# Smaller TensorE tiles and regrouped products in a hybrid decoder layer on one core

## Chip, cores and metric

The kernel runs on one core of a Trainium2 chip. The metric is the device time of one execution in microseconds (us). Three executions of the kernel before took 877.32, 881.16 and 882.83 us; the median is 881.16 us.

## The reference, cut to what matters

One layer of a decoder is computed for a prompt of 1024 tokens and for 8 sample sequences of 8 tokens each. The normalised input is projected once, and three groups of heads use the result:

- **RWKV-7** (4 heads of 64): a matrix state per head is updated token by token. With `S` the state, each step computes `sa = S @ (-kk)`, then `S = S*w + sa (kk*a)^T + v k^T`, and the output `y = S @ r`.
- **MLA** (8 heads): causal attention over the prompt. For the samples, attention over 2048 cached positions per sequence and over the sequence's own 8 new tokens: `s_past` and `s_new` are concatenated before the softmax.
- **Memory cross-attention** (4 heads): not touched here.

The gated outputs go through one output projection, a residual and a final RMSNorm. All inputs and outputs are float32.

## The kernel before

**Order of the work.** The program is written as Python generators that are stepped in turn, but what each engine runs in which order is set at compile time by a planner. It takes the instructions with the priority of their emission, holds one back while its operands or its buffer are not ready by the planner's own estimate of time, and fills in with others. So one engine's order in the trace is not the order of the file: products of different lines are found mixed.

**The RWKV part** (`rwkv_seg`, called from `phase_a`). The prompt is cut into 8 segments of two 64-token chunks, and the samples make a ninth of one chunk. Two head pairs (`hp`) times two chunks (`ch`) give the four index pairs `HP`, counted by `c`. A head pair fills 128 partitions; `H[0]` are partitions 0 to 63, `H[1]` 64 to 127, and `G` is the same in reverse. Three segments are in work at a time, in three stages (the `yield`s). Stage 1 computes the scores `AS` of keys against keys and queries (L742 to L750): per half `h`, four products of 64 rows by 128 columns, 128 moving columns each, into one PSUM bank (tag `rwa`, one buffer), then a VectorE multiply with the mask. A triangular inverse follows (L753 to L785, on VectorE and GpSimd, and L809 to L828 with 64x64 products). Stage 3 carries the state from chunk to chunk: `pW` from L846 and L850, `W`, `pU` from L856, `VU`, `pS` from L863, the next `S`. Then the outputs `py` (bank tag `rwd`, one buffer) are summed from a "tokens" product (L883, 128 rows by 64 columns) and a "state" product (L885, 64 by 64), pair by pair of `HP`, the two parts in alternating order, and normalised (L890 to L899), transposed (L903) and stored.

A product of two float32 operands shows in the trace as two passes: two weight loads and two matmuls. The tile shape of a matmul is the number of rows and of columns of the 128x128 array that it uses, 64*128 for instance.

While RWKV runs, TensorE also has other work: the input projection (`chunks` and `natural`, lines L181 to L183 of the helper `mm3`), and from about 400 us on the first two head pairs of the prompt's MLA.

**Prompt MLA** (`mla_prompt`). For each of four head pairs and each block `qb` of 128 queries, `scores` computes for each head `a` the scores against the keys up to the block's end, `n = 128 (qb+1)`. They are cut into parts of up to 512 keys, one bank each: three products per part (L1410 to L1412, float32r, at least 256 columns wide), a mask product on the last part (L1414), a VectorE maximum per part (L1415), a ScalarE exponential with a sum per part (L1420). For `n = 640` the parts are 512 and 128 keys, and the second is computed 256 wide. `outputs` transposes (L1440) and multiplies with `V` (L1451).

**Sample MLA** (`mla_sample`). The scores of the new tokens (L1211 to L1215) are made once: for each of four pairs of sequences, two products of 128 rows by 64 columns and then one of 64 by 128, all into one bank. Then 16 rounds over the cached pages follow, with scores (L1259 to L1261) and outputs (L1272) each.

Of the kernel before, what the change touches and what calls it, by code (L numbers as in the profile page):

```python
# [18 lines left out]
P = 128  # L19
# [684 lines left out]
def rwkv_seg(tc, A, g, sp, ps, s):  # L704
# [4 lines left out]
    nc = tc.nc  # L709
# [5 lines left out]
    n2 = 2 * nch  # L715
    mi = 1 if smp else 0
    T = lambda shape, tag, bufs=1, dt=F32: sp.tile(shape, dt, name="r_" + tag, tag=tag, bufs=bufs)
    bank = lambda tag="rwb": ps.tile([P, 512], F32, name="rwps", tag=tag, bufs=1)
    ga = lambda t, n: t.rearrange("p (a n) -> p a n", n=n)
    H = (slice(0, 64), slice(64, 128))  # L720
    G = H[::-1]
    HP = [(hp, ch) for hp in range(2) for ch in range(nch)]


    i, c0, t0 = (4, 0, 0) if smp else (s // 2, 2 * (s % 2), 128 * (s % 2))
    tok = SEQ if smp else s * N
    KR = T([P, 2, 2, 128], "KR", 3)[:, :, :nch]
    nc.sync.dma_start(out=KR, in_=g.kr_d[i, :, :, c0:c0 + nch])
    KN = T([P, 2, 2, 128], "KN", 2)[:, :, :nch]
# [10 lines left out]


    AS = T([P, 2, 4, 128], "AS", 3)[:, :, :n2]  # L742
    pa = [ga(bank("rwa"), 128) for h in range(2)]
    for c, (hp, ch) in enumerate(HP):
        for h in range(2):
            nc.tensor.matmul(pa[h][:, c], lhsT=KN[H[h], hp, ch], rhs=KR[H[h], hp, ch], start=True, stop=True)
    m = r.maskA[:, mi].rearrange("p a t -> p (a t)")
    for h in range(2):
        nc.vector.tensor_tensor(out=AS[:, h], in0=pa[h][:, :n2], in1=m.unsqueeze(1).broadcast_to([P, n2, 128]),
                                op=ALU.mult)  # L750


# [5 lines left out]
    for h in range(2):  # L758
        nc.vector.scalar_tensor_tensor(out=F[G[h], :n2], in0=AS[G[h], h, :, 32:64], scalar=r.bm[G[h], 4:5],
                                       in1=AS[G[h], h, :, 0:32], op0=ALU.mult, op1=ALU.add)  # L760
# [11 lines left out]
    for i in range(1, 16):  # L772
        n = i + 1
        nc.vector.tensor_tensor(out=tmp[:, :, :, :n], in0=NAv[:, i, :, :n].unsqueeze(2).broadcast_to([P, 2, 2, n]),  # L774
                                in1=Tl[:, :, :, :n].rearrange("p c b t -> p b c t"), op=ALU.mult)
# [5 lines left out]
    for b in range(4):  # L781
        nc.gpsimd.tensor_scalar(
            out=Tm[:, :, b * 16:(b + 1) * 16].rearrange("p c (r a) -> p r a c", a=2),
            in0=Tc.rearrange("p a r c -> p r a c")[:, :, :, :n2], scalar1=r.bm[:, b:b + 1], scalar2=1.0,
# [4 lines left out]
    VU = T([P, 2, 4, 64], "VU", 2)[:, :, :n2]  # L789
# [16 lines left out]
    fl = lambda t: t.rearrange("p a n -> p (a n)")  # L806
# [25 lines left out]
    if smp:  # L832
        py = rwkv_sample_state(tc, A, g, bank, T, KR, nat, AS, VU, Z)
    Ss = []
    for ch in range(0 if smp else nch):
        S = r.S
        q = 2 * s + ch
# [5 lines left out]
        for hp in range(2):  # L843
            c = hp * nch + ch
            for h in range(2):
                nc.tensor.matmul(pW[G[h], hp], lhsT=AS[H[h], h, c, 0:64], rhs=VU[H[h], h, c], start=True,  # L846
                                 stop=S is None)
# [5 lines left out]
        for hp in range(2):  # L853
            c = hp * nch + ch
# [5 lines left out]
        for hp in range(2):  # L860
            c = hp * nch + ch
# [10 lines left out]
        Ss.append(S)  # L872
    if not smp:
        py = ga(bank("rwd")[:, :64 * n2], 64)
        for c, (hp, ch) in enumerate(HP):

            S = Ss[ch]
            parts = ["tokens", "state"] if S is not None else ["tokens"]
            for k, part in enumerate(parts[::-1] if c % 2 else parts):
                a, b = k == 0, k == len(parts) - 1  # L880
                for h in range(2):
                    if part == "tokens":
                        nc.tensor.matmul(py[H[h], c], lhsT=AS[:, h, c, 64:128], rhs=VU[:, h, c], start=a, stop=b)  # L883
                    else:
                        nc.tensor.matmul(py[H[h], c], lhsT=KR[H[h], hp, ch, 64:128], rhs=S[H[h], hp], start=a,  # L885
                                         stop=b)

    st, mv = T([P, 4, 6], "st", 2), T([P, 4, 2], "mv", 2)
    yn = T([P, 4, 64], "yn", 2)
# [255 lines left out]
def mla_sample(tc, A, g, sp, banks):  # L1145
    nc = tc.nc
    bank = lambda: banks("ps", 1)
    obank = lambda: banks("po", 1)
    ident = g.ident
    fl = lambda t: t.rearrange("p h t -> p (h t)")  # L1150
# [19 lines left out]
    for hp in range(4):  # L1170
        w = sp.tile([P, 2, 256], F32, name="swq", tag="a2", bufs=4)
        nc.sync.dma_start(out=w, in_=A["wuq"][:, hp])
        for a in range(2):
            for k in range(2):
                nc.tensor.matmul(pq[:, a, hp], lhsT=w[:, k, a * P:(a + 1) * P], rhs=g.cqs[:, k], start=k == 0,
                                 stop=k == 1)
# [7 lines left out]
    qlat = sp.tile([P, 8, 8, 8], F32, name="sqlat")  # L1184
# [3 lines left out]
    for a in range(2):  # L1188
        pp = bank()
        nc.tensor.matmul(pp[:, :256], lhsT=sel[:, a], rhs=Q[:, a].rearrange("p h n -> p (h n)"), start=True, stop=True)  # L1190
        for rep in range(4):
            q, i = slice(rep * 32, rep * 32 + 32), rep % 2
# [17 lines left out]
    ps = bank()  # L1210
    for q in range(4):  # L1211
        for i in range(2):
            b, rows = 2 * q + i, slice(i * 64, i * 64 + 64)
            nc.tensor.matmul(ps[rows, q * 64:(q + 1) * 64], lhsT=fl(qlat[:, b]), rhs=g.cks, start=True, stop=False)
        nc.tensor.matmul(ps[:, q * 64:(q + 1) * 64], lhsT=qrf[0:64, q], rhs=g.kps, start=False, stop=True)  # L1215
    nc.vector.tensor_tensor(out=Pn, in0=ps[:, :256].rearrange("p (a b) -> p a b", a=4), in1=smask, op=ALU.add)
    nc.vector.tensor_reduce(out=nm[:, :, 4], in_=Pn, axis=AX.X, op=ALU.max, negate=True)
    pt = bank()
# [85 lines left out]
def mla_prompt(tc, A, g, sp, ps, more):  # L1304
# [4 lines left out]
    def bank():  # L1309
        turn[0] += 1  # L1310
        if more and turn[0] % 2:
            return more[0].tile([P, 512], F32, name="mT", tag="mT2", bufs=1)
        return ps.tile([P, 512], F32, name="mT", tag="mT", bufs=1)
# [31 lines left out]
    for hp in range(4):  # L1345
# [46 lines left out]
        def scores(qb):  # L1392
            c = slice(qb * P, (qb + 1) * P)
            n = (qb + 1) * P
            nm = sp.tile([P, 2, 3], F32, name="mnm", tag="mnm", bufs=3)
            sm = sp.tile([P, 2, 3], F32, name="msm", tag="msm", bufs=3)
            nh = (n + 511) // 512
            r = 2 if nh == 2 else 0
            Pts = []
            for a in range(2):  # L1400
                Pt = sp.tile([P, SEQ], F32, name="mP", tag="mP", bufs=3)
                S = []
                for i in range(nh):
                    c0 = i * 512
                    m = min(512, n - c0)
                    w = slice(c0, c0 + max(256, m))
                    s = sbank()
                    o = s[:, :max(256, m)]
                    last = i == nh - 1
                    nc.tensor.matmul(o, lhsT=qh[a][:, c], rhs=kh[a][:, w], start=True, stop=False)  # L1410
                    nc.tensor.matmul(o, lhsT=qh[a][:, c], rhs=kl[a][:, w], start=False, stop=False)  # L1411
                    nc.tensor.matmul(o, lhsT=ql[a][:, c], rhs=kh[a][:, w], start=False, stop=not last)  # L1412
                    if last:
                        nc.tensor.matmul(s[:, m - P:m], lhsT=idb, rhs=cmb, start=False, stop=True)  # L1414
                    nc.vector.tensor_reduce(out=nm[:, a, i:i + 1], in_=s[:, :m], axis=AX.X, op=ALU.max, negate=True)  # L1415
                    S.append((s, c0, m))
                if nh == 2:
                    nc.vector.tensor_tensor(out=nm[:, a, 2:3], in0=nm[:, a, 0:1], in1=nm[:, a, 1:2], op=ALU.min)  # L1418
                for i, (s, c0, m) in enumerate(S):
                    nc.scalar.activation(out=Pt[:, c0:c0 + m], in_=s[:, :m], func=AF.Exp, bias=nm[:, a, r:r + 1],  # L1420
                                         accum_out=sm[:, a, i:i + 1])
                Pts.append(Pt)
            if nh == 2:
                nc.vector.tensor_tensor(out=sm[:, :, 2], in0=sm[:, :, 0], in1=sm[:, :, 1], op=ALU.add)
            sm = sm[:, :, r]
            nc.vector.reciprocal(out=sm, in_=sm)
            rb = sp.tile([P, 2, 64], F32, name="mrb", tag="mrb", bufs=2)
            (nc.gpsimd if hp < 3 else nc.vector).tensor_copy(out=rb, in_=sm.unsqueeze(2).broadcast_to([P, 2, 64]))
            return Pts, rb
# [257 lines left out]
```

## Time and profile before

| what | us |
|---|---|
| median of three executions | 881.16 |
| the profiled execution | 879.73 |
| its span, first to last instruction | 878.1 |
| TensorE (PE) matmuls busy | 804.4 |
| TensorE weight loads (PEld) busy | 656.2 |
| VectorE (DVE) busy | 557.4 |
| ScalarE (ACT) busy | 366.8 |
| GpSimd (POOL) busy | 324.4 |

The profiled execution's span is 1.6 us shorter than its own time, and its time lies 1.4 us below the median. The busy time of an engine is the union of its instructions' durations. Matmuls are pipelined: the duration of one is from its start until its result is written, so several are under way at once, and what one costs TensorE is read from the distance between starts. The mean granted TensorE clock of the span is 0.968 of full speed.

### The profile page before, as it was taken

Reading aid. Unit: us, or ns where it says so; the run is one execution under the profiler, and the core shown is the slowest. Engines: PE = TensorE matmul, PEld = TensorE weight load, DVE = VectorE, ACT = ScalarE, POOL = GpSimd, SP = SyncE. Lnnn points to the kernel's source line nnn. Section 1 sums busy time; section 2 is a strip of 40 time slices with the busy share of each in tenths; the row PEclk is TensorE's granted clock in tenths of the full one; section 3 lists DMA queues with packets and bytes.
Section 4 is the critical chain, followed back from the end, with each engine's and each line's share of the span. In section 5 each row is a group of like instructions: output and inputs, shape, how many; then the busy total and the mean of one; then the engine's idle time right before and its main releaser. Section 6 shows DMA issues by size and latency. Waiting matters only on the chain. (4 is left out here: it accounts for less than half of the span.)

```text
span 878.1 us, 18102 instructions
## 1 busy us (share of the span) xinstructions
PE 804.4 (92%) x6284; PEld 656.2 (75%) x6284; DVE 557.4 (63%) x1342; ACT 366.8 (42%) x928; POOL 324.4 (37%) x597
## 2 busy tenths in 40 slices
PE   6999999988999999997899999998999989997992
PEld 6999999877899978876677766765666657765672
DVE  6844444499976787567968675455755567454553
ACT  7613233353432235555445534344544344341342
POOL 1411302286653435662523142526553422210132
PEclk9999999999999989999999999699999989999997
DMA  8643634845346121114202004725675667658462
GB/s 279 196 134 110 180 110 125 285 142 167 113 150 216 54 66 54 46 49 155 69 16 72 27 23 122 222 83 152 181 222 165 182 205 205 195 153 268 137 223 97
DMA packets 110621, 124.03 MB, mean 141 GB/s; under 512 B 26489, under 2 KB 85049, under 8 KB 110530
## 3 DMA queue, kind: packets, MB, share of 16 engines
q1 hardware_dynamic: 106434, 112.39, 41.5%
q0 software_dynamic: 4096, 10.49, 4.4%
q8 instruction: 50, 0.82, 0.4%
q14 instruction: 41, 0.34, 0.1%
HBM read 88.26 MB, written 34.58 MB: 140 GB/s over the span
## 5 line engine op out<-in xcount | busy, mean ns | idle before, releaser
L183 PE MATMUL mm<-xh,wwl 128*128 128x384 f32 (+1 forms) x336 | 111.8, 333 | 0.0
L181 PE MATMUL mm<-xh,wwh 128*128 128x384 f32 (+1 forms) x336 | 111.8, 333 | 0.0
L182 PE MATMUL mm<-xl,wwh 128*128 128x384 f32 (+1 forms) x336 | 111.2, 331 | 0.0
L1420 ACT ACTIVATE mP<-mS,mnm 128x512 f32<-128x512 f32 (+3 forms) x96 | 55.2, 579 | 56.3 <-DVE mnm L1418 34.3
L1415 DVE TENSOR_REDUCE mnm<-mS 128x1 f32<-128x512 f32 (+3 forms) x96 | 52.2, 553 | 32.3 <-PE mS L1412 20.1
L182 PEld LDWEIGHTS mm<-xl,wwh 128*128 128x128 f32 x336 | 63.2, 188 | 1.7 <-issue 0.8
L181 PEld LDWEIGHTS mm<-xh,wwh 128*128 128x128 f32 x336 | 63.2, 188 | 1.5 <-issue 0.6
L183 PEld LDWEIGHTS mm<-xh,wwl 128*128 128x128 f32 x336 | 63.2, 188 | 1.5 <-issue 0.6
L1451 PE MATMUL mO<-mPT,V 128*64 128x128 f32 x576 | 55.9, 284 | 0.1
L1440 PE MATMUL mT<-ident,mP 128*128 128x128 f32 x288 | 51.9, 292 | 3.3 <-ACT mP L1420 2.5
L1250 POOL DMA_DIRECT2D pg<-in_pool x64 | 34.9, 547 | 46.9 <-issue 43.1
L1451 PEld LDWEIGHTS mO<-mPT,V 128*64 128x64 f32 x576 | 37.0, 136 | 13.6 <-issue 9.0
L1444 ACT COPY mPT<-mT 128x512 f32<-128x512 f32 (+3 forms) x60 | 28.8, 480 | 42.2 <-PE mT L1440 41.5
L1440 PEld LDWEIGHTS mT<-ident,mP 128*128 128x128 f32 x288 | 34.8, 148 | 15.0 <-issue 4.6
L1410 PE MATMUL mS<-keh,qeh 128*128 128x512 f32 (+2 forms) x96 | 42.5, 443 | 1.3 <-ACT mP L1420 0.8
L1239 POOL DMA_INDIRECT pkr<-in_kpeT,rix x32 | 33.1, 1034 | 10.0 <-issue 7.7
L1567 DVE TENSOR_TENSOR px<-op,px 128x512 f32<-128x512 f32 x32 | 22.0, 689 | 21.9 <-PE op L183 18.8
L774 DVE TENSOR_TENSOR r_tmp<-r_NA,r_Tl 128x8 f32<-128x8 f32 (+4 forms) x135 | 33.3, 247 | 4.0 <-POOL r_NA L767 1.4
L1412 PE MATMUL mS<-keh,qel 128*128 128x512 f32 (+2 forms) x96 | 35.4, 368 | 0.0
L1411 PE MATMUL mS<-kel,qeh 128*128 128x512 f32 (+2 forms) x96 | 35.1, 366 | 0.0
L316 ACT ACTIVATE th<-g 128x384 f32<-128x384 f32 (+1 forms) x24 | 12.0, 505 | 48.0 <-DVE g L314 32.5
L181 PE MATMUL op<-wo,ph 128*128 128x512 f32 x64 | 27.6, 432 | 4.5 <-DVE px L1567 4.5
(447 smaller groups left out, 2240.3 us busy)
## 6 DMA issues: line engine op xcount, KB each, us to landing
pg<-in_pool SPq DMA_DIRECT2D x64, 128.0 KB, 2.8
pg<-in_pool POOLq DMA_DIRECT2D x64, 128.0 KB, 3.3
xp_d<-px SPq DMA_DIRECT2D x32, 256.0 KB, 3.6
wo<-in_wout SPq DMA_DIRECT2D x8, 512.0 KB, 4.8
px<-in_xn SPq DMA_DIRECT2D x16, 256.0 KB, 3.3
px<-xp_d SPq DMA_DIRECT2D x16, 256.0 KB, 3.5
o_keh<-xp_d SPq DMA_DIRECT2D x8, 512.0 KB, 5.1
out_y_prompt<-o_kel SPq DMA_DIRECT2D x16, 256.0 KB, 2.5
```

What stands on the lines that cost most here:

```text
L181: nc.tensor.matmul(out, lhsT=lh, rhs=rh, start=start, stop=False)
L182: nc.tensor.matmul(out, lhsT=lh, rhs=rl, start=False, stop=False)
L183: nc.tensor.matmul(out, lhsT=ll, rhs=rh, start=False, stop=stop)
L774: nc.vector.tensor_tensor(out=tmp[:, :, :, :n], in0=NAv[:, i, :, :n].unsqueeze(2).broadcast_to([P, 2, 2, n]), in1=Tl[:, :, :, :n].rearrang ...
L1250: eng.dma_start(out=t[:, j], in_=A["pool"][ds(v, 1)].rearrange("o p c -> (o p) c"))
L1410: nc.tensor.matmul(o, lhsT=qh[a][:, c], rhs=kh[a][:, w], start=True, stop=False)
L1411: nc.tensor.matmul(o, lhsT=qh[a][:, c], rhs=kl[a][:, w], start=False, stop=False)
L1412: nc.tensor.matmul(o, lhsT=ql[a][:, c], rhs=kh[a][:, w], start=False, stop=not last)
L1415: nc.vector.tensor_reduce(out=nm[:, a, i:i + 1], in_=s[:, :m], axis=AX.X, op=ALU.max, negate=True)
L1420: nc.scalar.activation(out=Pt[:, c0:c0 + m], in_=s[:, :m], func=AF.Exp, bias=nm[:, a, r:r + 1], accum_out=sm[:, a, i:i + 1])
L1440: nc.tensor.transpose(pt[:, (k - k0) * P:(k - k0 + 1) * P], Pts[a][:, k * P:(k + 1) * P], ident)
L1451: nc.tensor.matmul(po[a * 64:a * 64 + 64, 1, qb % 2], lhsT=V[:, k, v:v + 64], rhs=PTs[k // 4 * 2 + a][:, k % 4 * P:(k % 4 + 1) * P], start ...
```

## The change

In three places the same sums are computed from other products or in another order.

- `rwkv_seg`, scores: each 64-by-128 product becomes two 64-by-64 products, one for each half of the output's partitions, with the same moving operand; a bank is now asked for inside the loop over `h`.
- `rwkv_seg`, outputs: first all "tokens" products of the four pairs, then all "state" products. One start flag (on `c == 0`) and one stop flag now serve all four accumulations of the bank.
- `mla_sample`, new-key scores: first the eight products of 128 by 64, then the four of 64 by 128, again with one start and one stop for the bank.
- `mla_prompt`, `scores`: for `n = 640` the parts are 384 and 256 keys; for all other `n` they stay.

```diff
     AS = T([P, 2, 4, 128], "AS", 3)[:, :, :n2]
-    pa = [ga(bank("rwa"), 128) for h in range(2)]
-    for c, (hp, ch) in enumerate(HP):
-        for h in range(2):
-            nc.tensor.matmul(pa[h][:, c], lhsT=KN[H[h], hp, ch], rhs=KR[H[h], hp, ch], start=True, stop=True)
     m = r.maskA[:, mi].rearrange("p a t -> p (a t)")
     for h in range(2):
-        nc.vector.tensor_tensor(out=AS[:, h], in0=pa[h][:, :n2], in1=m.unsqueeze(1).broadcast_to([P, n2, 128]),
+        pa = ga(bank("rwa"), 128)
+        for c, (hp, ch) in enumerate(HP):
+            for o in H:
+                nc.tensor.matmul(pa[o, c], lhsT=KN[H[h], hp, ch, o], rhs=KR[H[h], hp, ch], start=True, stop=True)
+        nc.vector.tensor_tensor(out=AS[:, h], in0=pa[:, :n2], in1=m.unsqueeze(1).broadcast_to([P, n2, 128]),
                                 op=ALU.mult)
...
         py = ga(bank("rwd")[:, :64 * n2], 64)
-        for c, (hp, ch) in enumerate(HP):
-
-            S = Ss[ch]
-            parts = ["tokens", "state"] if S is not None else ["tokens"]
-            for k, part in enumerate(parts[::-1] if c % 2 else parts):
-                a, b = k == 0, k == len(parts) - 1
+
+        for part in range(2):
+            for c, (hp, ch) in enumerate(HP):
+                S = Ss[ch]
                 for h in range(2):
-                    if part == "tokens":
-                        nc.tensor.matmul(py[H[h], c], lhsT=AS[:, h, c, 64:128], rhs=VU[:, h, c], start=a, stop=b)
-                    else:
-                        nc.tensor.matmul(py[H[h], c], lhsT=KR[H[h], hp, ch, 64:128], rhs=S[H[h], hp], start=a,
-                                         stop=b)
+                    if part == 0:
+                        nc.tensor.matmul(py[H[h], c], lhsT=AS[:, h, c, 64:128], rhs=VU[:, h, c], start=c == 0,
+                                         stop=False)
+                    elif S is not None:
+                        nc.tensor.matmul(py[H[h], c], lhsT=KR[H[h], hp, ch, 64:128], rhs=S[H[h], hp], start=False,
+                                         stop=c == n2 - 1)
...
-            nc.tensor.matmul(ps[rows, q * 64:(q + 1) * 64], lhsT=fl(qlat[:, b]), rhs=g.cks, start=True, stop=False)
-        nc.tensor.matmul(ps[:, q * 64:(q + 1) * 64], lhsT=qrf[0:64, q], rhs=g.kps, start=False, stop=True)
+            nc.tensor.matmul(ps[rows, q * 64:(q + 1) * 64], lhsT=fl(qlat[:, b]), rhs=g.cks, start=q == 0, stop=False)
+    for q in range(4):
+        nc.tensor.matmul(ps[:, q * 64:(q + 1) * 64], lhsT=qrf[0:64, q], rhs=g.kps, start=False, stop=q == 3)
...
+            parts = [(0, 384), (384, 640)] if n == 640 else [(c0, min(n, c0 + 512)) for c0 in range(0, n, 512)]
...
-            nh = (n + 511) // 512
+            nh = len(parts)
...
-                for i in range(nh):
-                    c0 = i * 512
-                    m = min(512, n - c0)
+                for i, (c0, c1) in enumerate(parts):
+                    m = c1 - c0
```

## Rows read from the trace of the kernel before

**Rows 1.** Page, busy time by engine: busy us, share of the span, instructions.
```profile
PE 804.4 (92%) x6284; PEld 656.2 (75%) x6284; DVE 557.4 (63%) x1342; ACT 366.8 (42%) x928; POOL 324.4 (37%) x597
```
**Rows 2.** Windows: stretch, length, busy (instructions) per engine, PE clock, DMA share, GB/s.
```profile
260.00:545.00 285.00, 270.35 (x2827) 219.11 (x2825) 202.35 (x687) 129.20 (x361) 114.69 (x254) 0.97 0.25 73
380.00:440.00 60.00, 49.30 (x535) 39.14 (x533) 45.59 (x151) 31.71 (x87) 26.20 (x57) 0.94 0.31 93
545.00:800.00 255.00, 234.31 (x1597) 168.70 (x1596) 148.63 (x314) 107.77 (x271) 95.88 (x163) 0.95 0.62 181
```
**Rows 3.** Waits of PE, 380 to 440 us: who, for what, total us, times, longest.
```profile
PE rwps L792 <- DVE r_AS L749: 2.4, 1, 2.4
```
**Rows 4.** PE timeline, one score group: start us, us to the last end, line, shape, count.
```profile
335.72 1.16 PE L746 MATMUL rwps<-r_KR,r_KN 64*128 64x128 f32 x8
336.80 0.46 PE L181 MATMUL mm<-nh,xh 128*128 128x416 f32 x1
```
**Rows 5.** PE timeline, sample outputs: 64-column tiles with 128 moving columns.
```profile
629.09 1.09 PE L1272 MATMUL spo<-pg,spPT 128*64 128x128 f32 x16
630.11 0.33 PE L1440 MATMUL mT<-ident,mP 128*128 128x128 f32 x1
```
**Rows 6.** PE timeline, state products of two lines side by side, 416 us.
```profile
416.13 0.22 PE L850 MATMUL rwps<-r_S,r_KR 64*64 64x64 f32 x1
416.14 0.22 PE L885 MATMUL rwps<-r_S,r_KR 64*64 64x64 f32 x1
416.14 0.22 PE L850 MATMUL rwps<-r_S,r_KR 64*64 64x64 f32 x1
...
416.19 0.22 PE L850 MATMUL rwps<-r_S,r_KR 64*64 64x64 f32 x1
```
**Rows 7.** PE timeline, end of one segment's outputs, 421 us.
```profile
421.09 0.45 PE L885 MATMUL rwps<-r_S,r_KR 64*64 64x64 f32 x8
421.47 0.34 PE L883 MATMUL rwps<-r_VU,r_AS 128*64 128x64 f32 x4
421.74 0.50 PE L181 MATMUL mS<-lath,wuqh 128*128 128x512 f32 x1
```
**Rows 8.** PE timeline, score groups beside 64*64 work, the first and the last.
```profile
283.97 0.33 PE L846 MATMUL rwps<-r_VU,r_AS 64*64 64x64 f32 x4
284.23 1.16 PE L746 MATMUL rwps<-r_KR,r_KN 64*128 64x128 f32 x8
...
431.42 1.16 PE L746 MATMUL rwps<-r_KR,r_KN 64*128 64x128 f32 x8
432.51 0.68 PE L813 MATMUL rwps<-r_Z,r_Pm 64*64 64x64 f32 x16
```
**Rows 9.** PE timeline, new-key scores, from the first to what follows the last.
```profile
575.93 0.33 PE L1214 MATMUL sps<-cks,sqlat 128*64 128x64 f32 x4
...
578.43 0.33 PE L1451 MATMUL mO<-mPT,V 128*64 128x128 f32 x2
```
**Rows 10.** PE timeline, prompt scores 512 and 384 wide.
```profile
448.70 0.39 PE L1411 MATMUL mS<-kel,qeh 128*128 128x512 f32 x1
448.93 0.40 PE L1412 MATMUL mS<-keh,qel 128*128 128x512 f32 x1
...
475.41 0.34 PE L1411 MATMUL mS<-kel,qeh 128*128 128x384 f32 x1
475.58 0.33 PE L1412 MATMUL mS<-keh,qel 128*128 128x384 f32 x1
```
**Rows 11.** Groups by shape, ScalarE exponentials by width: busy us, mean ns, idle before.
```profile
L1420 ACT ACTIVATE mP<-mS,mnm 128x512 f32<-128x512 f32 x48 | 32.9, 687 | 41.6 <-DVE mnm L1418 34.3 <-DVE mnm L1415 5.9 <-POOL r_rs L896 0.5
...
L1420 ACT ACTIVATE mP<-mS,mnm 128x384 f32<-128x384 f32 x16 | 9.2, 578 | 4.7 <-DVE r_Tl L776 2.3 <-DVE msm L1426 2.3
L1420 ACT ACTIVATE mP<-mS,mnm 128x256 f32<-128x256 f32 x16 | 7.5, 470 | 3.0 <-DVE mnm L1415 1.6 <-DVE msm L1426 1.5
L1420 ACT ACTIVATE mP<-mS,mnm 128x128 f32<-128x128 f32 x16 | 5.8, 364 | 6.9 <-DVE mnm L1415 6.9
```

## The prediction, made before the changed kernel ran

> **What bounds the kernel now.** I read the busy times first: TensorE is busy for 92% of the span, the next engine for 63% [rows 1]. An average over stages proves nothing, so next come the windows. The RWKV part, where two of the edits lie, runs from 260 to 545 us. TensorE is busy for 270.35 of these 285 us, VectorE, the next, for 202.35 [rows 2]. Nearly all that TensorE misses is in one minute part: from 380 to 440 us it is busy for 49.30 of 60 us, so 10.7 of the 14.65 us of idling are there [rows 2]. There the input projection has run out and the recurrence waits for itself; the longest single wait is 2.4 us for VectorE's mask multiply [rows 3]. In the other 225 us the other engines keep up, and what TensorE is spared should end the stage sooner. From 545 to 800 us, the rest of the MLA, it is busy for 234.31 of 255 us [rows 2]: still the busiest, but one part in twelve is waiting.
>
> The third view is the timeline, since "busy" here is not speed. Two things are to be seen in it: the distance between starts within one shape, and what happens where the shape changes.
>
> **Price of a change of shape.** Pairs of 64-column passes with 64 moving columns start 0.06 us apart [rows 6], so four pairs of state products should hold TensorE 0.24 us and two pairs of tokens products 0.12. At the end of a segment, where they stand between other shapes, they hold it 0.38 and 0.27 us (21.09 to 21.47 to 21.74 after 400 us) [rows 7]. Each visit to a shape thus costs about **0.15 us** beyond its passes, and I price each boundary between two shapes that goes at 0.15.
>
> **Scores in quadrants.** Now a group of eight passes, 64 rows by 128 columns, takes 1.08 us from its first start to the next line's first (335.72 to 336.80) [rows 4]. The new group has sixteen passes of 64 by 64, with the same 128 moving columns. No row shows this form, so I bound it.
> - Lower end: the two column halves run side by side. The sample outputs do this with 128 rows: sixteen passes of 64 columns and 128 moving ones take 629.09 to 630.11, 1.02 us [rows 5].
> - Upper end: the halves take turns, since both read the same 64 rows. Then it is twice as much, 2.04 us.
>
> I take 1.02. For it speaks that products of L850 and L885, which pairwise read the same rows and write opposite halves, start within 0.01 us of each other, and the next of L850 comes 0.06 later, as if it were alone [rows 6].
>
> A rule of the Trainium skill speaks against it (TensorE: Matmul & The Clock Gate, "The mechanism" in Part 3): weight loads overlap with matmuls in flight only where the row group differs. Both halves have the same row group, and by that rule the upper end would hold, 0.96 us more per group in place of 0.06 less; the sixteen passes of the sample outputs, which share all rows, disagree with it [rows 5].
>
> There are seventeen full groups (two in each of eight segments, two half ones for the samples): 17 x 0.06 = **1.0 us**. More comes from neighbours. I counted 23 visits of this shape, since some groups are split, and at 20 of their 46 edges stands 64-by-64 work, from the visit at 284.23 us to the one at 431.42 [rows 8]. With the same shape these boundaries go: 20 x 0.15 = **3.0 us**. VectorE's multiply reads the same 512 columns as before: nothing.
>
> **Outputs by shape.** No product is added or dropped. Now a segment ends state, tokens [rows 7], because the last pair's order is reversed; I counted eight such lone visits of the tokens shape, and six of the state shape earlier in the segments (first-chunk state products between a 128-by-64 run and something else). Grouped, each takes one boundary with it: 14 x 0.15 = **2.1 us**. Bounds: nothing, if the planner splits them anew, and 28 x 0.15 = 4.2, if each visit takes both its boundaries. The state products now wait behind the last tokens product, but only the normalisation of `py` waits for them, which is off the chain of the state; its cover is the next segment's work, and where that is missing (380 to 440 us) a segment ends some 0.4 us later, the length of the state visit [rows 7]. The `rwd` bank is not read sooner or later by more than that.
>
> **New-key scores.** Now 575.93 to 578.43, 2.50 us, for four rounds of two shapes [rows 9], so seven boundaries within. Grouped there is one: 6 x 0.15 = **0.9 us**.
>
> **640 keys in 384 and 256.** Three products per head and head pair, eight times, shrink from 512 to 384 columns; the second part was computed 256 wide already. Starts lie 0.23 us apart at 512 and 0.17 at 384 [rows 10]: 24 x 0.06 = **1.4 us**. The exponentials take 687 + 364 = 1051 ns now and 578 + 470 = 1048 then [rows 11]; I put the maxima, as many columns as before, at nothing too.
>
> **Sum.** 1.0 + 3.0 + 2.1 = 6.1 us in the RWKV part, 2.3 us after it. Of the first I let 225/285 arrive (the part outside 380 to 440 us), 4.8; of the second, with its waits for pages and weights, two thirds, 1.5. That is **6.3 us** off the profiled execution's 879.73: 873.4. That execution lies 1.4 us below the median of the three; I take half of this, and forecast **874 us**, 0.8% under 881.16. The bounds of the terms give 865 to 880: all 8.4 us and the other 2.1 of the outputs paid in full, or the outputs' and the neighbours' 5.1 us not at all.
>
> **Rivals.** A measurement of this kernel tells 1% from no change, 8.8 us: under 872.3 is faster, over 890.0 slower.
>
> *The halves take turns (slower).* At L746 each group costs 0.96 us more, 17 x 0.96 = 16.3; the other 7.4 us still come, three quarters of them paid, 5.5. That is +10.8 us, 890 to 892. It decides from 0.37 us per group on (6.3/17), when a pair of halves is some 0.05 us longer than the 0.13 of now. Against it stand rows 5 and 6. Chance 0.06.
>
> *A new stall (slower).* The planner arranges everything anew, and the recurrence could be left without filling work at one more place. A second stretch like 380 to 440 us, with 10.7 us idle and the clock at 0.94 (2.4 GHz fell to 1.2 for some 7 us of it, after TensorE's idling) [rows 2], would give 874 + 11 to 14 = 885 to 888; two of them 897. Chance 0.06.
>
> *The stretch closes (much faster).* The same the other way: shorter groups let the recurrence run ahead, or filling work falls there. Of its 10.7 us of idling up to 9 go: 865. Chance 0.12.
>
> *The time turns into waits.* TensorE is spared 6 us, but the state chain and the pages' transfers end when they did; only a quarter arrives, 879. The 92% speak against it, the single waits [rows 3] for it. Chance 0.14.
>
> *It does not do what it says.* The planner splits the groups as it split L746 into 23 visits, so the shapes change as often as now. Then 1.0 + 0.9 + 1.4 remain, 2.5 us paid, 878. Chance 0.12.
>
> **Numbers.** The forecast has 0.50, and its own range, 868 to 880, lies half on either side of 872.3: 0.24 faster, 0.26 the same. With the closed stretch faster has 0.36. The same has 0.26 + 0.14 + 0.12, and 0.02 from a single mild stall: 0.54. Slower has 0.10. The range 865 to 887 leaves out the worst of the two slow cases and the best of the closed stretch.
>
> **What would show it.** Right: L746 appears as 64*64, sixteen passes in about 1.0 us, the halves starting 0.01 apart; fewer boundaries between shapes from 260 to 545 us, by some 30; L883 and L885 in one run each at a segment's end; the new-key scores in 1.6 us; L1411 at 640 keys followed after 0.17. The stretch 260 to 545 us, up to the first sample products, ends some 5 us sooner. Wrong: a group of L746 near 2 us, as many boundaries as before, or TensorE's idling grown by what its work shrank; a shift of several us from granted clock or idling at a place that no edit touches would make the sum right and the time wrong.

## The result and the profile after

The changed kernel takes 869.29 us, the median of four runs (867.92 to 870.11). The kernel before took 881.16, 882.83, 877.32 and 894.41 us in the same comparison; the last of these was a disturbed run, and the ratio leaves it out: **0.9872**, 95% interval 0.9829 to 0.9914. So the time fell by 1.3%, with an interval of 0.9% to 1.7%. The profiled execution took 870.11 us with a span of 868.4, against 879.73 and 878.1 before: 9.6 us less.

Lines moved a little: the scores are L748 now, the tokens products of the outputs L881, their state products L884, the new-key scores L1213 and L1215.

The page of the changed kernel, its busy times; they answer to [rows 1].

```profile
PE 795.1 (92%) x6420; PEld 650.5 (75%) x6420; DVE 555.1 (64%) x1342; ACT 365.6 (42%) x928; POOL 329.7 (38%) x597
```

TensorE has 136 more instructions, seventeen groups with eight more passes each, and is busy for 9.3 us less. Its idling is the same: 878.1 - 804.4 = 73.7 us before, 868.4 - 795.1 = 73.3 after. The other engines do what they did.

The windows of the changed kernel, with the columns of [rows 2]: stretch, length, busy us (instructions) of TensorE, its weight loads, VectorE, ScalarE and GpSimd, then TensorE's clock, the DMA share and GB/s.

```profile
260.00:545.00 285.00, 264.94 (x2977) 219.04 (x2976) 203.32 (x694) 130.13 (x365) 125.28 (x267) 0.98 0.28 82
380.00:440.00 60.00, 49.91 (x683) 40.09 (x681) 51.54 (x180) 29.86 (x81) 29.73 (x63) 0.91 0.31 93
545.00:800.00 255.00, 235.42 (x1611) 166.36 (x1610) 148.00 (x313) 106.80 (x268) 90.85 (x151) 0.97 0.60 180
```

Three things are to be seen. From 380 to 440 us TensorE is as idle as before, 10.1 us against 10.7: the stretch did not close. From 545 to 800 us, where no line of the recurrence runs, the clock is 0.97 where it was 0.95. And the first window holds more than before, since the sample work begins earlier: the first sample product starts at 537.31 us, before at 549.10. From the first scores to that product TensorE idles for 16.5 us (before 16.1), behind it for 41.5 (42.4). So more than half of the idling lies behind the recurrence, in both kernels.

Busy time is not work, as the clock changes what a microsecond does. Taking half of the time off in which TensorE was busy at 1.2 in place of 2.4 GHz leaves its work at the full clock (an estimate: in the kernel before, passes of 384 columns start 0.32 us apart at the lower level and 0.17 at the higher): 804.4 - 20.6 = 783.8 us before and 795.1 - 17.2 = 777.8 after. So of the 9.7 us of span **6.0 are work**, 3.4 are clock and 0.4 idling. Of the 6.0, 1.5 us lie ahead of the first RWKV product (248.0 against 246.5), where both kernels run the same 1662 passes and no edit acts; behind it 4.5 are left.

The timeline of TensorE in the changed kernel, one lone score group: start, us to the last end, line, shape, passes. It answers to [rows 4].

```profile
271.50 1.09 PE L748 MATMUL rwps<-r_KR,r_KN 64*64 64x128 f32 x16
272.52 0.42 PE L181 MATMUL mm<-xh,wwh 128*128 128x320 f32 x1
```

The group takes 1.02 us, as do the five others that stand alone. In the trace the passes start in pairs, 0.007 us apart, and the pairs 0.109 us. By the code all sixteen read the same 64 rows (one `h`), so passes that share their rows do run side by side; that a pair is the two column halves is inferred, since the trace does not name the half. The rule that was weighed (the Trainium skill, TensorE: Matmul & The Clock Gate, "The mechanism" in Part 3) would have them take turns; these rows disagree with it.

The same view at 330 us: what becomes of the other groups.

```profile
329.93 0.32 PE L748 MATMUL rwps<-r_KR,r_KN 64*64 64x128 f32 x1
329.93 0.33 PE L856 MATMUL rwps<-r_W,r_Z 64*64 64x64 f32 x2
330.09 0.27 PE L748 MATMUL rwps<-r_KR,r_KN 64*64 64x128 f32 x1
330.10 0.31 PE L856 MATMUL rwps<-r_W,r_Z 64*64 64x64 f32 x3
330.21 0.25 PE L902 MATMUL rwps<-ident,r_yn 64*64 64x64 f32 x1
...
331.36 0.49 PE L748 MATMUL rwps<-r_KR,r_KN 64*64 64x128 f32 x5
```

The scores have the shape of the recurrence's other products now, and the planner puts them among these, in one visit to the 64-by-64 shape. Before they stood as blocks of their own [rows 8]. The score lines now stand in 17 visits to their shape, not 23.

The same view at the end of a segment; it answers to [rows 7].

```profile
349.67 0.27 PE L881 MATMUL rwps<-r_VU,r_AS 128*64 128x64 f32 x1
349.68 0.27 PE L863 MATMUL rwps<-r_VU,r_nat 128*64 128x64 f32 x1
...
350.06 0.46 PE L881 MATMUL rwps<-r_VU,r_AS 128*64 128x64 f32 x9
350.44 0.68 PE L884 MATMUL rwps<-r_S,r_KR 64*64 64x64 f32 x16
351.06 0.33 PE L543 MATMUL ax<-ident,cn 128*128 128x128 f32 x1
```

All sixteen passes of the state products are one run, and the last tokens products share a visit with a line of their shape, L863.

The new-key scores in the changed kernel; they answer to [rows 9].

```profile
565.90 0.33 PE L1213 MATMUL sps<-cks,sqlat 128*64 128x64 f32 x2
566.32 0.59 PE L1518 MATMUL op<-wo,pm 128*64 128x512 f32 x1
566.75 0.63 PE L1213 MATMUL sps<-cks,sqlat 128*64 128x64 f32 x14
567.31 1.10 PE L1215 MATMUL sps<-kps,sqr 64*128 64x64 f32 x8
568.34 0.33 PE L1432 MATMUL mO<-ident,mrb 128*128 128x128 f32 x1
```

The products lie by shape; other work of 0.43 us stands among them. Without it they take 2.01 us where they took 2.50.

The 640-key scores and the exponentials of the changed kernel, from the timeline and from the groups by shape; they answer to [rows 10, 11].

```profile
450.19 0.34 PE L1411 MATMUL mS<-kel,qeh 128*128 128x384 f32 x1
450.36 0.33 PE L1412 MATMUL mS<-keh,qel 128*128 128x384 f32 x1
```

```profile
L1420 ACT ACTIVATE mP<-mS,mnm 128x512 f32<-128x512 f32 x40 | 27.4, 688 | 31.4 <-DVE mnm L1418 18.3 <-DVE mnm L1415 8.0 <-issue 4.5
L1420 ACT ACTIVATE mP<-mS,mnm 128x384 f32<-128x384 f32 x24 | 13.9, 580 | 13.1 <-DVE mnm L1418 8.8 <-DVE mnm L1415 2.1 <-DVE r_Tl L776 1.6
```

Eight exponentials moved from 512 to 384 columns, and the spacing at 384 is 0.17 us as read before.

Last the waits of TensorE from 530 to 870 us: whom it waited for, us in total, times, the longest. First the kernel before, then the changed one.

```profile
PE op L181 <- DVE px L1567: 5.3, 5, 2.4
PE sps L1267 <- ACT spP L1264: 4.5, 2, 3.8
PE sps L1259 <- DMA pg<-in_pool: 4.0, 2, 2.2
```

```profile
PE sps L1259 <- DMA pg<-in_pool: 10.4, 6, 4.5
PE op L181 <- DVE px L1567: 3.2, 2, 1.6
...
PE sps L1267 <- ACT spP L1264: 0.3, 1, 0.3
```

The samples begin earlier, and 6.4 us more are spent waiting for pages of the cache; nearly as much is won at the two other places (2.1 and 4.2). None of these lines was edited.

### The profile page after: what moved, and what is told of

Its sections match the earlier page's. It is cut to its first block, busy times and chain, and to the rows that moved or that the text cites. A ratio compares the mean times of both kernels' runs of the same rounds, so it can differ in the third digit from the quotient of the medians.

```text
span 868.4 us, 18384 instructions
## 1 busy us (share of the span) xinstructions
PE 795.1 (92%) x6420; PEld 650.5 (75%) x6420; DVE 555.1 (64%) x1342; ACT 365.6 (42%) x928; POOL 329.7 (38%) x597
## 5 line engine op out<-in xcount | busy, mean ns | idle before, releaser
L1451 PE MATMUL mO<-mPT,V 128*64 128x128 f32 x576 | 52.7, 286 | 0.5 <-ACT mPT L1444 0.4
L1440 PEld LDWEIGHTS mT<-ident,mP 128*128 128x128 f32 x288 | 33.0, 141 | 18.1 <-ACT mP L1420 5.2
L1410 PE MATMUL mS<-keh,qeh 128*128 128x512 f32 (+2 forms) x96 | 39.3, 410 | 0.8 <-ACT mP L1420 0.6
L1259 PE MATMUL sps<-pg,sqlat 128*64 128x512 f32 x64 | 24.6, 620 | 11.0 <-DMA pg<-in_pool 10.4
L1412 PE MATMUL mS<-keh,qel 128*128 128x512 f32 (+2 forms) x96 | 33.3, 347 | 0.0
L1411 PE MATMUL mS<-kel,qeh 128*128 128x512 f32 (+2 forms) x96 | 33.2, 346 | 0.0
```

Of the source, the lines that this page charges most:

```text
L1440: nc.tensor.transpose(pt[:, (k - k0) * P:(k - k0 + 1) * P], Pts[a][:, k * P:(k + 1) * P], ident)
L1451: nc.tensor.matmul(po[a * 64:a * 64 + 64, 1, qb % 2], lhsT=V[:, k, v:v + 64], rhs=PTs[k // 4 * 2 + a][:, k % 4 * P:(k % 4 + 1) * P], start ...
```

## Experiments

Two explanations are weighed. **The work**: time fell by what TensorE was spared. **The plan**: the planner lays the whole kernel out anew at each edit, and the new layout happened to wait less, or to keep the clock up more, than the old one. By the first, single edits add up, and an edit that spares nothing moves nothing. By the second, neither holds.

All runs in one table. The time is the median of the executions that the ratio rests on. The ratio is to the kernel before on the same chip; idle is span less busy; "clock" is half of the busy time at the lower clock level; "work" is busy less "clock"; changes are the boundaries between two shapes on TensorE in the whole trace. The four columns behind the ratio are of one execution, the profiled one, and that need not be a typical one: e4's is the fastest of its ten (863.27 us), f2's the fastest and e5's the slowest of their six (864.63 and 874.57).

The clock moves between executions of one and the same kernel. The 49 executions of the kernel before that the experiments' ratios rest on have mean granted clocks from 0.954 to 0.978 (mean 0.967) and times from 885.55 to 871.62 us; the four of the changed kernel have 0.965 to 0.972 (mean 0.969). So one execution does not show that the 3.4 us of clock between the two profiled ones, or the other differences in that column, come from the layout.

| kernel | us | ratio [95%] | idle | clock | work | changes |
|---|---|---|---|---|---|---|
| before | | 1 | 73.7 | 20.6 | 783.8 | 471 |
| after | 869.29 | 0.9872 [0.9829, 0.9914] | 73.3 | 17.2 | 777.8 | 401 |
| e1_quadrants | 857.93 | 0.9781 [0.9724, 0.9838] | 54.5 | 21.6 | 778.1 | 425 |
| e2_outputs | 869.66 | 0.9896 [0.9859, 0.9932] | 64.4 | 21.2 | 782.3 | 437 |
| e4_tail | 870.34 | 0.9896 [0.9860, 0.9932] | 65.7 | 13.8 | 782.1 | 467 |
| e5_turns | 869.19 | 0.9886 [0.9838, 0.9934] | 68.6 | 24.4 | 779.9 | 393 |
| e8_scores_outputs | 867.51 | 0.9872 [0.9840, 0.9905] | 68.0 | 18.0 | 781.1 | 421 |
| e7_noout | 866.69 | 0.9857 [0.9818, 0.9896] | 63.7 | 33.3 | 771.2 | 415 |
| e6_noquad | 862.77 | 0.9806 [0.9761, 0.9851] | 61.3 | 19.6 | 780.1 | 430 |
| n3_transp | 867.56 | 0.9884 [0.9846, 0.9922] | 66.8 | 17.6 | 782.2 | 466 |
| n4_rev | 873.04 | 0.9941 [0.9910, 0.9973] | 69.3 | 18.3 | 785.6 | 477 |
| n5_both | 873.03 | 0.9917 [0.9875, 0.9959] | 70.7 | 12.6 | 788.1 | 470 |
| f1_after_transp | 865.22 | 0.9819 [0.9773, 0.9864] | 65.8 | 20.2 | 778.4 | 428 |
| f2_scores_transp | 871.20 | 0.9891 [0.9842, 0.9940] | 62.9 | 16.2 | 783.9 | 455 |

### One edit at a time

**e1_quadrants**: the kernel before with the scores alone changed.

```diff
-    pa = [ga(bank("rwa"), 128) for h in range(2)]
...
+        pa = ga(bank("rwa"), 128)
+        for c, (hp, ch) in enumerate(HP):
+            for o in H:
+                nc.tensor.matmul(pa[o, c], lhsT=KN[H[h], hp, ch, o], rhs=KR[H[h], hp, ch], start=True, stop=True)
```

> The kernel before with the scores in quadrants alone. Theory A (boundaries: the gain is 0.15 us for each boundary between tile shapes that goes, plus 0.06 us per score group): 40 to 48 edges of the 64*128 shape go, some come back as edges of 64*64, so 20 to 30 boundaries fewer from the first score to the first sample product; 4 to 5.5 us less there, 876 to 878 us against 882. Theory B (luck of the new order: any edit is planned anew, and waits and granted clock move by several us whatever the boundaries): the time lies anywhere from 868 to 890, and the change of idling and clock is larger than 0.15 us times the boundaries.

Measured 0.9781: 2.2% faster, more than the whole change. Its work fell by 5.7 us, which is near the change's 6.0; 19.2 us came from idling. Where they came from is read in the windows of e1_quadrants, with the columns of [rows 2], and the last window of the kernel before.

```profile
265.00:545.00 280.00, 264.25 (x2926) 216.74 (x2922) 200.78 (x688) 129.79 (x361) 118.38 (x259) 0.94 0.26 79
545.00:800.00 255.00, 243.83 (x1657) 172.15 (x1657) 151.54 (x319) 109.22 (x272) 89.67 (x155) 0.99 0.65 194
800.00:870.00 70.00, 40.09 (x170) 29.41 (x168) 29.29 (x48) 20.84 (x48) 15.85 (x29) 0.90 0.35 117
```

```profile
800.00:870.00 70.00, 54.58 (x226) 39.96 (x226) 35.73 (x56) 23.65 (x52) 16.88 (x30) 0.97 0.56 189
```

From 545 to 800 us TensorE is busy for 243.83 us at a clock of 0.99, where the kernel before has 234.31 at 0.95 [rows 2]; that is 9.5 us less idling. Another 9.3 lie behind 800 us: up to the end of its span TensorE idles for 14.2 us there (54.3 less 40.09), before for 23.5 (78.1 less 54.58). No line that runs there was edited. Over the whole span the clock gave nothing: from 265 to 545 us it was 0.94, where the kernel before has 0.97 from 260 on. Its waits from 530 us on show the same from the other side: the largest is 4.1 us, and the pages, 10.4 us in the changed kernel, cost 2.2.

```profile
PE mS L1410 <- ACT mP L1420: 4.1, 3, 3.6
PE sps L1259 <- DMA pg<-in_pool: 2.2, 2, 1.6
```

**e2_outputs**: the outputs alone.

```diff
-            for k, part in enumerate(parts[::-1] if c % 2 else parts):
...
+        for part in range(2):
+            for c, (hp, ch) in enumerate(HP):
```

> The kernel before with the outputs grouped by shape alone. Theory A: 14 to 25 boundaries fewer in the RWKV part, 2 to 4 us less there, 878 to 880 us against 882. Theory B: a change of more than 5 us either way, or one without a change in the number of boundaries.

Measured 0.9896, about 9 us, with 34 shape changes less but only 1.5 us less work. The grouped state products may lose something too: before, 29 of the 120 passes of L885 start within 0.02 us of a pass of another line, L850 for instance [rows 6]; in e2 it is 2 of 120. What that costs was not measured. The rest of its gain is idling, 9.3 us less.

**e4_tail**: the new-key scores and the 640 keys alone.

```diff
+    for q in range(4):
+        nc.tensor.matmul(ps[:, q * 64:(q + 1) * 64], lhsT=qrf[0:64, q], rhs=g.kps, start=False, stop=q == 3)
...
+            parts = [(0, 384), (384, 640)] if n == 640 else [(c0, min(n, c0 + 512)) for c0 in range(0, n, 512)]
```

> The kernel before with the new-key scores grouped and 640 keys cut in 384 and 256, nothing else. Theory A: 0.9 us of boundaries and 1.4 us of columns, two thirds of it seen: 880 to 881 us against 882, and no change before 425 us, since these lines run later. Theory B: the RWKV part or the MLA part changes by more than 4 us though TensorE has only 2.3 us less to do.

Measured 0.9896. Its timeline has the new-key scores without anything between:

```profile
568.62 0.63 PE L1214 MATMUL sps<-cks,sqlat 128*64 128x64 f32 x16
569.18 1.10 PE L1216 MATMUL sps<-kps,sqr 64*128 64x64 f32 x8
570.22 0.55 PE L1441 MATMUL mT<-ident,mP 128*128 128x128 f32 x3
```

That is 568.62 to 570.22, **1.60 us**, the predicted figure to the hundredth. But the work fell by 1.7 us in all, where the span of its profiled execution is 16.5 us shorter: 8.0 us are idling and 6.8 clock, in an execution 7.1 us faster than e4's median. The three single edits give 2.2 + 1.0 + 1.0 = 4.2% together; all of them at once give 1.3%. They don't add, and that speaks against the work as the only cause.

### Two of three

**e8_scores_outputs** is e1 and e2 together, **e7_noout** e1 and e4: the diffs above, joined.

> The two RWKV edits together, without the new-key scores and the 640 keys. Theory A: net TensorE work some 1.7 us above the changed kernel's 777.8 (that is what the tail edits took off alone), 779 to 780, and a time some 1.5 us above its 869. Theory B: the time is anywhere from 857 (the scores alone) to 880, set by the idling after 540 us.

> The changed kernel with the outputs as before (scores in quadrants, new-key scores grouped, 384 and 256 keys). Theory A: net work 1 to 2 us above 777.8 or the same, since the outputs alone took off 1.5, and a time of 870 to 871. If the grouped outputs themselves are what holds the changed kernel 11 us above the scores alone, it comes out near 856; if that is luck of the plan, anywhere from 856 to 875.

Measured 0.9872 and 0.9857. Adding the outputs or the two small edits to the scores made e1 slower by about 1%, each of which alone had made the kernel faster by 1%. The work does not explain it: e8's 781.1 us are above the 779 to 780 that theory A gave, and its time is below. (For e7 the split of busy time is rough: 33.3 us to the clock is the largest of all, and its work of 771.2 is then too low to be believed.)

### Another order of the same work

**n3_transp**: the kernel before, with two blocks of stage 1 exchanged. The transposes of the values and the copies behind them are emitted ahead of those of the keys. No product is added, dropped or reshaped.

```diff
-    pn = ga(bank("rwa")[:, :n2 * 128], 128)
-    for c, (hp, ch) in enumerate(HP):
-        nc.tensor.transpose(pn[:, c], KN[:, hp, ch], ident)
...
     pv = ga(bank("rwa")[:, :256], 128)
...
+    pn = ga(bank("rwa")[:, :n2 * 128], 128)
+    for c, (hp, ch) in enumerate(HP):
+        nc.tensor.transpose(pn[:, c], KN[:, hp, ch], ident)
```

> The kernel before with the same work, only written in another order: in the first stage of an RWKV segment the transposes of the values stand ahead of those of the keys. No product, shape or column changes. Theory A (the time follows the work: boundaries of shape and columns): 876 to 881 us, within 0.3% of the kernel before (878.6). Theory B (any edit is planned anew, and idling and granted clock move the time by as much as the edits did): more than 5 us away from it, at the same TensorE work net of clock, 783 to 785 us.

Measured **0.9884**, interval 0.9846 to 0.9922: as much as the change itself, with nothing spared (466 shape changes against 471, work 782.2 against 783.8). The windows of n3_transp, from 545 to 800 us:

```profile
545.00:800.00 255.00, 234.21 (x1618) 166.50 (x1616) 149.81 (x315) 107.86 (x271) 96.01 (x161) 0.98 0.64 193
```

TensorE is as busy as in the kernel before, 234.21 against 234.31 us, at a clock of 0.98 against 0.95 [rows 2]. The larger part of the gain is not the clock: over the whole span the clock took 17.6 us against 20.6, and TensorE idles for 6.9 us less.

**n4_rev**: the kernel before, with the alternation of the outputs begun the other way round. **n5_both**: n3 and n4.

```diff
-            for k, part in enumerate(parts[::-1] if c % 2 else parts):
+            for k, part in enumerate(parts if c % 2 else parts[::-1]):
```

> The kernel before with the same work and the outputs' two parts in the opposite alternation (state before tokens for the first pair). As many tokens and state products as before, shapes alternate as often. Theory A: within 0.3% of the kernel before. Theory B: more than 5 us away, with idling and clock loss changed and the net TensorE work within 1.5 us of the 783.8 of before.

> The kernel before with both rewritings that change no work (transposes swapped, outputs in the opposite alternation). If the kernel before is an unlucky plan, this is once more below it, 867 to 875; if the first two were chance, 874 to 884.

Measured 0.9941 and 0.9917. Every other order of the old work that was run is faster than the kernel before, by 0.6 to 1.2%, and n5 is not the sum of n3 and n4.

### The change and the scores under another order

**f1_after_transp** is the changed kernel with n3's exchange, **f2_scores_transp** is e1 with it.

> The changed kernel with the values' transposes written ahead of the keys' (the edit without new work that took 1.2% off the kernel before). If that edit is good in itself, the two gains add: 0.987 x 0.988 = 0.975 of the kernel before, 857 us. If it only threw the dice again on an unlucky plan, the changed kernel moves by up to 8 us either way, 860 to 876. If the changed kernel's gain is the work alone, its plans scatter around 872 less 6, that is 866, as those of the old work scatter around 872.

> The scores in quadrants alone, with the same rewriting of the transposes. If 858 is what quadrants are worth, it stays within 5 us of 858. If 858 is a lucky plan, it goes back to the 864 to 870 of the other kernels with quadrants.

Measured 0.9819 and 0.9891. The exchange takes about 0.5% off the changed kernel, which the intervals don't tell from nothing, and adds 1.1% to e1. So at least half of the 2.2% of e1, the fastest kernel of the study, belongs to its layout: with its scores kept and two blocks exchanged it is level with n3 (0.9884), which has the old scores. Nor is the work less there: 783.9 us with quadrants in f2, 782.2 without in n3.

### The scores' form

**e6_noquad**: the changed kernel with passes of 128 columns in place of two halves.

```diff
-            for o in H:
-                nc.tensor.matmul(pa[o, c], lhsT=KN[H[h], hp, ch, o], rhs=KR[H[h], hp, ch], start=True, stop=True)
+            nc.tensor.matmul(pa[:, c], lhsT=KN[H[h], hp, ch], rhs=KR[H[h], hp, ch], start=True, stop=True)
```

> The changed kernel with the scores as 64 by 128 products again, so outputs grouped, new-key scores grouped, 384 and 256 keys. By the work it lacks the larger part of the gain: 4 to 6 us above the changed kernel's 867, 871 to 873. By the plan alone it is anywhere from 858 to 876.

Measured 0.9806. Its groups take 1.08 us again (264.90 to 265.98) and there are 29 more shape changes than in the changed kernel, 2.3 us more work; it measured 0.7% faster all the same (0.9806 against 0.9872, with intervals that overlap), since TensorE idles for 12.0 us less. By this pair alone the quadrants would have cost time.

```profile
264.90 1.16 PE L747 MATMUL rwps<-r_KR,r_KN 64*128 64x128 f32 x8
265.98 0.45 PE L181 MATMUL mm<-xh,wwh 128*128 128x384 f32 x1
```

**e5_turns**: the changed kernel with all eight passes of one half written ahead of the eight of the other.

```diff
-        for c, (hp, ch) in enumerate(HP):
-            for o in H:
+        for o in H:
+            for c, (hp, ch) in enumerate(HP):
```

> The changed kernel, but within a score group first all products of the lower output half and then all of the upper, so that neighbours in the queue are on the same half. If the halves run side by side only when they alternate, a group takes 1.7 to 2.0 us in place of 1.02, 0.7 to 1.0 more for 17 groups: 12 to 17 us more than the 869 of the changed kernel, 881 to 886. If TensorE overlaps them in any order, or if the time of a group does not matter for the end, 867 to 872.

Measured 0.9886, the same as the changed kernel within the intervals. The timeline of e5_turns, one lone group:

```profile
271.97 1.58 PE L748 MATMUL rwps<-r_KR,r_KN 64*64 64x128 f32 x16
273.48 0.42 PE L181 MATMUL mm<-xh,wwh 128*128 128x320 f32 x1
```

It takes 1.51 us against 1.02, not the 2.04 of the upper bound. The single starts in the trace show how: four passes begin one by one, 0.109 to 0.160 us apart, then eight within 0.38 us, two series of the same spacing that overlap, then four alone again. Which quadrants the overlapping ones are in, the trace doesn't say. Seven of the seventeen groups stand alone in this kernel (1.46 to 1.51 us), so some 7 x 0.49 = 3.4 us are added to TensorE, and up to 17 x 0.49 = 8.3; the profile has 2.1 us more work, with the scatter told below. The time shows none of it.

### What the runs say together

Four layouts of the old work have been run (before, n3, n4, n5): mean ratio 0.9936, from 0.9884 to 1. Two of the whole changed work (after, f1): mean 0.9846. The difference is **0.9%, or 7.9 us** of 879. With a scatter of 0.5% from one layout to the next, the standard error of that difference is about 0.4% (0.5 x the root of 1/4 + 1/2). So the times alone make a gain likely and do not show it. In the same kernels the work at full clock is 784.9 and 778.1 us in the mean, 6.8 us less, with a scatter of 2.6 us among the old. Part of this scatter is the count's own: ahead of the first RWKV product all fourteen kernels run the same 1662 passes, and their work there comes out between 246.4 and 249.0 us. Counted behind that point alone, the difference is 5.8 us.

The kernel before, e1, e2, e4, e6, e7, e8 and the changed kernel are all eight combinations of three edits (scores, outputs, the two small ones together). So each edit has four pairs of kernels that differ in it alone. In the mean of its pairs the scores take off 0.5%, the outputs 0.2% and the small ones 0.3%, but each has pairs of either sign (minus is faster): from -2.2 to +0.7%, -1.0 to +0.9% and -1.0 to +0.8%. With the scatter of 0.5% a mean of four pairs has a standard error of some 0.35%, so none of the three is told from nothing by its time.

So both explanations hold a part. The change spares work, by some 6 us; that is a mean over layouts. What one edit does to the time of one kernel is this plus or minus 4 to 5 us from the layout, and the kernel before is the slowest of all layouts that were run: one more order of the old work takes 0.6 to 1.2% off. Where the layouts differ is in the idling behind the first sample product: 42.4 us in the kernel before, 41.5 in the changed one, 38.7 in n3, 34.0 in e6 and 25.4 in e1. From the first RWKV product up to there it is 11.2 to 16.5 us in all fourteen.

## Why the prediction was right, and where not

The forecast was 874.0 us, the range 865 to 887, and the result, 869.29, lies in it, 4.7 us under the forecast. It falls among the cases of more than 1% faster, which had 0.36; 0.54 stood on a smaller difference. By its own steps:

**What bounds the kernel.** Held for this pair: TensorE's share of 92% did not change, its idling neither (73.7 and 73.3 us), and the span fell by what its busy time fell by. But the prediction looked for idling in the RWKV part, 14.65 us, and most lies behind it (42.4 us); other layouts remove up to 17 us of that.

**Price of a change of shape.** Too simple. In the whole trace there are 70 boundaries less, from the first scores to the first sample product 58 (226 runs of one shape against 284), where 40 had been counted (20 at the scores, 14 + 6). At 0.15 us 70 would have been 10.5 us, but all the work spared was 6.0, and 2.4 of it has other sources (1.0 and 1.4 by passes). A boundary that goes saved about 0.05 us, or the grouping cost something that the count doesn't see; e2's 34 boundaries with 1.5 us speak for the same size, e1's 46 with 4.7 us for 0.10. No run here separates the two.

**Scores in quadrants.** Right to the digit: 1.08 became 1.02. The passes start in pairs, and the rival in which the halves take turns was wrong; with one half written ahead of the other (e5) the price was 0.49 us and not 0.96. That neighbours would join the same visit was right as well [rows 8]. The work fell by 5.7 us in e1 where 1.0 + 3.0 had been forecast, but by 1.2 from e2 to e8 and by 2.3 from e6 to the changed kernel, and from n3 to f2 it rose by 1.7: of the 3.0 no run shows how much came.

**Outputs by shape.** Mis-sized: 2.1 us forecast, 1.5 measured as work in e2, within the bounds of 0 to 4.2; from e1 to e8 the same edit comes with 3.0 us more, so the size lies within the scatter. The last visits of a segment came out as forecast. Not foreseen was that the old order let state products run beside others, as [rows 6] shows, the very rows from which the price of the quadrants was read.

**New-key scores and 640 keys.** Right: 1.60 us in e4, 0.17 us of spacing, exponentials 580 + 471 = 1051 ns against 1051. In the changed kernel the planner put 0.43 us of other work among the new-key products, and 0.41 of the 0.9 us is lost to that (2.01 against 1.60).

**Sum.** The terms came to 8.4 us of TensorE's work, 6.3 of them paid as time. Measured are 6.0 us of work in this pair and some 6 over layouts, so the mechanism held and the terms were too large, above all the price of a boundary. The profiled time fell by 9.6 us all the same, since 3.7 came from clock and idling that no term has. That the time lies near the forecast is in part luck: too much work in the sum, and nothing for the rest. The sum's bounds are also miscounted: 8.4 and 2.1 us paid in full give 869 to 871 us, not 865, and without the 5.1 us it is 876 to 878, not 880. The measured time is at the lower edge of that narrower range.

**Rivals.** Of the "new stall", the "stretch that closes" and the "time that turns into waits" none came as described: from 380 to 440 us TensorE idles as before. But what they have in common, that time moves at places that no edit touches, is what the other 3.7 us are made of: 3.4 of clock and 0.4 of idling. Whether the clock's part is the layout's or this execution's is open. "It does not do what it says" was wrong: 17 visits, not 23.

**The weakest step** is what follows from the sentence "The planner arranges everything anew". The prediction priced this at single, rare events (0.06 and 0.12), and took the kernel before as a fair sample of its own work. It is not rare: each of the three orders of the old work shifted the time by 5 to 10 us, as much as the whole sum. The distribution of the forecast should have been as wide from this term as from all others together, and centred lower, had it been known that the layout before is a poor one; nothing in the rows of that one layout could tell. The end of the recurrence, forecast 5 us sooner, came 11.8 us sooner at the first sample product (13.5 less from the first scores on), and 2.1 of it was given back to the end. That is not all spared: between these two points the work fell by 11.0 us, and behind them it rose by 6.5, with 1847 passes there against 1809.

**What stays open.** How much of this one pair's 1.28% is the change and how much its layout: the trace's 6.0 us of work (4.5 behind the first RWKV product) is the best answer, and its scatter among layouts that do the same is 2.6 us. How much the work of one layout scatters from execution to execution was not measured. An experiment that holds the order of everything else fixed and changes the products alone was not made, since each edit is planned anew. Why the exchange helps one layout and hurts another is not settled either.

## What to carry to other kernels

Where a program orders the work, time an edit that spares nothing before you believe one that spares little: here two exchanged blocks gave 0.9884, and the change gave 0.9872. Judge an edit of one per cent over several layouts, by their times and by the work in the traces (busy time without what the clock took), and not by one pair: the same edit spared 5.7 us of work in one order and none in another. Products of a small shape given the shape of their neighbours share visits with them, 17 in place of 23 here; what that is worth in time was not shown.

## What the runs showed of the hardware

- Passes of 64 by 64 that read the same 64 rows, written for alternating column halves, start in pairs 0.007 us apart, and the pairs 0.109 us apart with 128 moving columns: sixteen take 1.02 us. With the eight of one half written ahead of the eight of the other they take up to 0.49 us more per group (e5_turns).
- Passes of 64 rows by 128 columns start 0.112 us apart, eight in 1.08 us, in the kernel before and in e6_noquad alike. The code of the kernel before alternates the two row halves, but the planner did not: the multiply of one half, which needs all four of its products, starts right behind the first eight passes, and the second eight come 4 us later. So rows that alternate were not run. Whether quadrants that alternate rows as well, four at once, would take less than 1.02 us was not tried.

```profile
264.63 1.13 PE L746 MATMUL rwps<-r_KR,r_KN 64*128 64x128 f32 x8 [0.28 <-DMA r_bv<-bv_d]
265.79 0.69 DVE L749 TENSOR_TENSOR r_AS<-rwps,c_maskA 128x512 f32<-128x512 f32 x1 [1.82 <-PE rwps L746]
269.89 1.16 PE L746 MATMUL rwps<-r_KR,r_KN 64*128 64x128 f32 x8
```
